# Residual additions, sums of squares and the last addition of a hybrid encoder step, moved from VectorE and GpSimd to accumulating DMAs

## The chip, the core and the metric

The kernel runs as one program on one core of a Trainium2 chip. The metric is device time in microseconds (us). The engines are named as the profile names them: PE is TensorE (matmul), DVE is VectorE, ACT is ScalarE, POOL is GpSimd, SP is SyncE, which only issues DMAs here. Each engine runs its own queue of instructions in order. A DMA is issued by one engine, which goes on to its next instruction, and it lands later.

## What is computed

One layer of a streaming encoder for 512 prompt tokens and 128 sample tokens (640 columns in all), width 2048. The parts that the change touches come after the mixer:

```
h = x + merged @ w_out
f = rms_norm(h, g_ffn)
h = h + (silu(f @ w_gate) * (f @ w_up)) @ w_down
gate = sigmoid(rms_norm(h, g_ple) @ w_ple_gate)
h = h + gate * (p_i @ w_ple_proj)
```

## The kernel before

Everything is held transposed: a tile has 128 features in its partitions and the 640 tokens in its free dimension, and a "pair" is two such tiles (128x2x640 float32, 640 KB). Pairs come from a pool of two buffers. DRAM scratch tensors (`h_dr`, `h2_dr`, `pj_dr`, `fc_dr`, `hc_dr`) hold what does not fit.

All large products are made by `strassen`: seven half-size products instead of eight, on float32 values that are cut into a high part (`wh`, `kf`) and a low remainder (`wl`). The work goes by weight units. A unit is one 512 KB load `wst` by SP. POOL makes three combinations of its blocks (lines L109, L110, L111 in `winograd_weights`), DVE a fourth (L112); ACT cuts the high part in two instructions (L86: one from `wst`, one from `ws`, the combinations), DVE subtracts to get the low part (L87), and PE runs 42 matmuls of 320 columns (L1205 to L1207). `ws` has one buffer and `wh` and `wl` two, so L109 of the next unit waits until L87 has read `ws`.

At the end of a product the seven sums are brought out of PSUM by ACT, DVE and POOL (L1232 to L1240). The last of these on DVE is L1239, which this text calls the last eviction.

The stages behind the mixer, in order:

- **Out-projection**, `o0` to `o7`, four units each. Behind each product: SP loads a pair of x, DVE adds it (L1280), ACT scales it by the gain (L1267, two instructions), POOL forms the combinations of the activations (L118 to L121), the pair goes to `h_dr`, ACT squares it (L1249) and DVE adds the two halves to a running sum `ssqa` (L1253, L1254).
- **Gate and up**, 22 times (`g`, `u`), eight units for both. After `g0` the sums of squares pass through two small matmuls `pm` over the partitions and a reciprocal root (`scale_rows`); after that `by_rows` multiplies every product by the row scale (L1257).
- **Down**, 28 cells: each of the eight pairs of h is built from several cells. The first 20 cells add their result to `h_dr` with an accumulating DMA issued by POOL (L1346). The last eight cells finish the pairs j = 4, 5, 6, 7 (three units each) and j = 0, 1, 2, 3 (two units each). Behind each, SP loads the pair from `h_dr`, DVE adds it (L1350), and scaling, combinations, squares and the write to `h2_dr` follow as in the out-projection.
- **Gate of the embedding**, `p0` to `p7`, four units each. After `p0` the row scale is made as above. Behind each of p0 to p6: `by_rows`, Sigmoid, the product with `pj` (L1370, DVE), a load of `hy` from `h2_dr`, its addition on POOL (L1373), and a write to the output `o_yT`.

The order of each engine's queue is chosen when the program is built, by a list scheduler of the framework that simulates the dependences; the code's order is only its input.

Of the kernel before, what the change touches and what calls it, by code (L numbers as in the profile page):

```python
# [9 lines left out]
F32 = mybir.dt.float32  # L10
# [4 lines left out]
OP = mybir.AluOpType  # L15
# [4 lines left out]
P = 128  # L20
D = 2048
KT = D // P
NTOK = 640
# [15 lines left out]
def halves(ap):  # L39
    return ap.rearrange("p (h n) -> p h n", h=2)  # L40
# [124 lines left out]
def hybrid_step(ctx: ExitStack, tc: tile.TileContext, io):  # L165
    nc = tc.nc
# [5 lines left out]
    dp = ctx.enter_context(tc.tile_pool(reuse_waits="tile", name="dram", bufs=1, space=DRAM))  # L172
# [22 lines left out]
    g_dr = dp.tile([1024, NTOK], F32, name="g_dr")  # L195
    m_dr = dp.tile([D, NTOK], F32, name="m_dr")
    h_dr = dp.tile([D, NTOK], F32, name="h_dr")
    h2_dr = dp.tile([D, NTOK], F32, name="h2_dr")
    tc_dr = dp.tile([FT // 2, P, 7, NH2], F32, name="tc_dr")
    fc_dr = dp.tile([KT // 2, P, 7, NH2], F32, name="fc_dr")  # L200
    hc_dr = dp.tile([KT // 2, P, 7, NH2], F32, name="hc_dr")
# [819 lines left out]
    for k in range(8):  # L1021
        t = gp_.tile([P, NTOK], F32, tag="xg", name=f"gld{k}", bufs=3)
# [4 lines left out]
    for k in range(2):  # L1027
        t = gp_.tile([P, NTOK], F32, tag="xg", name=f"p{k}", bufs=3)
# [3 lines left out]
    def row_scale(s, n, pm, y0, y2):  # L1032

        for i in range(2):
            nc.tensor.matmul(pm[i], ones, s[:, i * NH2 : (i + 1) * NH2], start=True, stop=True)
        for i in range(2):
            nc.vector.tensor_scalar(s[:, i * NH2 : (i + 1) * NH2], pm[i], 1.0 / n, EPS, op0=OP.mult, op1=OP.add)
        rsqrt(y0, y2, s, s)
# [7 lines left out]
    def rows(dram, j):  # L1046
        return dram[2 * j * P : 2 * (j + 1) * P, :].rearrange("(a p) n -> p a n", p=P)
# [92 lines left out]
    def bank(name):  # L1140
        return pc.tile([P, 512], F32, tag="p", name=name)

    def pair(name):
        return fo.tile([P, 2, NTOK], F32, tag="R", name=name, bufs=2)
# [19 lines left out]
    def seven(name):  # L1164
        return xp.tile([P, 7, NH2], F32, tag="c7", name=name, bufs=1)

    def keep(eng, c, dram, i):

        winograd_rows(eng, c[:, :4], c[:, 4:])
        nc.sync.dma_start(dram[i], c)  # L1170
# [72 lines left out]
    def scale_rows(s, n):  # L1243
        y = pair("y")
        pm = [bank(f"pm{i}")[:, :NH2] for i in range(2)]
        row_scale(s, n, pm, y[:, 0], y[:, 1])

    def squares(s, x, t, first, other=nc.vector):
        nc.scalar.activation(t, x, AF.Square)  # L1249
        if first:  # L1250
            nc.vector.tensor_tensor(s, t[:, 0], t[:, 1], op=OP.add)
        else:
            nc.vector.tensor_tensor(s, s, t[:, 0], op=OP.add)  # L1253
            other.tensor_tensor(s, s, t[:, 1], op=OP.add)  # L1254

    def by_rows(x, s):
        nc.vector.tensor_tensor(x, x, s[:, None, :].to_broadcast([P, 2, NTOK]), op=OP.mult)  # L1257
# [1 line left out]
    for i in range(5, 8):  # L1259
        s = seven(f"sm{i}")  # L1260
        mk.append(build(kp_tile(f"km{i}", i), pair(f"bm{i}"), s[:, 4:], m_dr, i, ssqs))
    ssqh, ssqp = ssqa, ssqs

    def scaled(c, x, gain, j):

        for a in range(2):
            nc.scalar.activation(c[:, 2 * a : 2 * a + 2], halves(x[:, a]), AF.Copy, scale=gain[:, 2 * j + a : 2 * j + a + 1])  # L1267

    fk = []
    for j in range(8):  # L1270
        after = None
        if j == 7:
            def after(u):
                for i in (2 * u, 2 * u + 1):
                    if i < 7:
                        fk.append(fetch(f"f{i}", i, fc_dr, i, nc.gpsimd if i == 3 else nc.vector, i == 6))
        r = strassen(f"o{j}", mk, after)
        x = pair(f"x{j}")
        nc.sync.dma_start(x, io["xT"][2 * j : 2 * j + 2].rearrange("a p n -> p a n"))
        nc.vector.tensor_tensor(r, r, x, op=OP.add)  # L1280
        c = seven(f"c{j}")
        scaled(c, r, gffn, j)
        if j < 7:
            keep(nc.gpsimd, c, fc_dr, j)
        else:
            winograd_rows(nc.gpsimd, c[:, :4], c[:, 4:])
            kf7 = kp_tile("kf7", 7)
            fk.append(kf7)
            later.setdefault(1, []).append(lambda: whole(kf7, c))
        nc.sync.dma_start(rows(h_dr, j), r)  # L1290
        squares(ssqh, r, x, j == 0)

    tk, slots = {}, (0, 1, 2, 3, 4, 5, 6, 7)

# [7 lines left out]
    for f in range(FT // 2):  # L1302
        z = strassen(f"g{f}", fk, cut_late if f == 0 else None)
        if f == 0:
            scale_rows(ssqh, D)
        by_rows(z, ssqh)
        nc.scalar.activation(z, z, AF.Silu)
        after = None
        if f == FT // 2 - 1:
            def after(u):  # L1310
                next_t(nc.gpsimd if u < 2 else nc.vector)
        c = seven(f"t{f}")
        t = c[:, :4].rearrange("p (a h) n -> p a (h n)", a=2)
        strassen(f"u{f}", fk, after, t)
        by_rows(t, ssqh)
        nc.vector.tensor_tensor(t, t, z, op=OP.mult)
        keep(nc.gpsimd, c, tc_dr, f)
# [14 lines left out]
    for n, (j, us, first, last) in enumerate(cells):  # L1332
        def after(i, us=us, n=n):
            uses[us[i]] -= 1
            if not uses[us[i]] and n < len(cells) - 8:
                next_t()
            if len(cells) - 4 <= n < len(cells) - 2:
                next_h()

        if n == len(cells) - 1:  # L1340
            def after(i):
                for _ in range(2 - i):
                    next_h()
        r = strassen(f"d{n}", [tk[i] for u in us for i in (2 * u, 2 * u + 1)], after)
        if not last:
            nc.gpsimd.dma_start(rows(h_dr, j), r, accum_op=OP.add)  # L1346
            continue
        x = pair(f"hx{j}")
        nc.sync.dma_start(x, rows(h_dr, j))
        nc.vector.tensor_tensor(r, r, x, op=OP.add)  # L1350
        c = seven(f"hc{j}")
        scaled(c, r, gple, j)
        if j != 3:
            keep(nc.gpsimd, c, hc_dr, j)
            ready.append(j)
        else:
            winograd_rows(nc.gpsimd, c[:, :4], c[:, 4:])
            hk[j] = whole(kp_tile("kh3", hslot[j]), c)
        nc.sync.dma_start(rows(h2_dr, j), r)
        squares(ssqp, r, x, j == 4)  # L1360
    hk = [hk[i] for i in (4, 5, 6, 7, 0, 1, 2, 3)]
    for j in range(7):
        z = strassen(f"p{j}", hk)
        if j == 0:
            scale_rows(ssqp, D)
        by_rows(z, ssqp)
        nc.scalar.activation(z, z, AF.Sigmoid)
        x = pair(f"pj{j}")
        nc.sync.dma_start(x, rows(pj_dr, j))
        nc.vector.tensor_tensor(z, z, x, op=OP.mult)  # L1370
        x = pair(f"hy{j}")
        nc.sync.dma_start(x, rows(h2_dr, j))
        nc.gpsimd.tensor_tensor(z, z, x, op=OP.add)  # L1373
        nc.sync.dma_start(rows(io["o_yT"], j), z)


    x = pair("pj7")
    y = seven("hy7")[:, :4].rearrange("p (a h) n -> p a (h n)", a=2)
    nc.sync.dma_start(x, rows(pj_dr, 7))
    nc.sync.dma_start(y, rows(h2_dr, 7))  # L1380
    ps = products("p7", hk, order=(1, 2, 6, 5, 3, 7, 4))
    z = pair("rp7")
    r11, r12, r21, r22 = blocks(z)
# [143 lines left out]
```

## Time and profile before

| | |
|---|---|
| median of three runs | 3040.45 us (3038.37 to 3044.05) |
| the profiled execution's own time | 3040.49 us |
| its span, first to last instruction | 3038.7 us |
| mean granted clock of TensorE | 0.977 of full speed |
| busy: PE | 2860.6 us, 94% of the span |
| busy: DVE | 2041.0 us, 67% |
| busy: POOL | 1541.0 us, 51% |
| busy: ACT | 1237.8 us, 41% |

A busy share is an average over stages with different limits, so the stages are also read one by one. Of the view by windows, each row names a stretch in us from the start of the span, then the busy time of each engine with the number of its instructions, then the granted clock, the busy share of the 16 DMA engines, and GB/s. The profiled execution ran 0.04 us from the median, so durations read from it can be set against the median as they are.

### The profile page before, as it was taken

Reading aid. Unit: us, or ns where it says so; the run is one execution under the profiler, and the core shown is the slowest. Engines: PE = TensorE matmul, PEld = TensorE weight load, DVE = VectorE, ACT = ScalarE, POOL = GpSimd, SP = SyncE. Lnnn points to the kernel's source line nnn. Section 1 sums busy time; section 2 is a strip of 40 time slices with the busy share of each in tenths; the row PEclk is TensorE's granted clock in tenths of the full one; section 3 lists DMA queues with packets and bytes.
Section 4 is the critical chain, followed back from the end, with each engine's and each line's share of the span. In section 5 each row is a group of like instructions: output and inputs, shape, how many; then the busy total and the mean of one; then the engine's idle time right before and its main releaser. Section 6 shows DMA issues by size and latency. Waiting matters only on the chain.

```text
span 3038.7 us, 48382 instructions
## 1 busy us (share of the span) xinstructions
PE 2860.6 (94%) x19051; PEld 2734.2 (90%) x19051; DVE 2041.0 (67%) x2827; ACT 1237.8 (41%) x1627; POOL 1541.0 (51%) x1548
## 2 busy tenths in 40 slices
PE   7899999999789889999999999999999999987898
PEld 6789988888788889999999999999889999987887
DVE  8949254454777786666666666666775666689666
ACT  4333365556633443333333333333434344344432
POOL 6512300000666665656565656565664555567555
PEclk9899999999899999999999999999999999999999
DMA  5465744456444623233333333332555455557343
GB/s 166 145 180 169 224 175 153 173 202 206 171 145 165 247 81 114 99 114 105 109 110 104 113 106 109 104 113 100 206 126 170 110 164 169 157 217 250 126 147 130
DMA packets 138069, 453.82 MB, mean 149 GB/s; under 512 B 14160, under 2 KB 34736, under 8 KB 124528
## 3 DMA queue, kind: packets, MB, share of 16 engines
q1 hardware_dynamic: 120608, 401.06, 38.7%
q0 software_dynamic: 15936, 45.47, 5.9%
q8 instruction: 149, 2.44, 0.3%
q10 hardware_dynamic: 1296, 4.20, 0.3%
q14 instruction: 80, 0.66, 0.1%
HBM read 344.55 MB, written 103.47 MB: 147 GB/s over the span
## 4 chain that ended last, share of the span: by engine, by line
POOL 22%; DVE 15%; PE 13%; issue 8%; ACT 5%; DMA 1%; DVEq 0%; POOLq 0%; SPq 0%; ACTq 0%
DVE wl L87 7%; POOL ws L110 7%; POOL ws L109 6%; ACT wh L86 5%; POOL ws L111 4%; PE d L1205 4%; PE d L1207 4%; PE d L1206 4%; POOL t L121 1%; DVE t L1257 1%; POOL t L118 1%; DVE rg L1257 1%; DVE kt L1051 1%; POOL rp L1373 1%; POOL t L119 1%
## 5 line engine op out<-in xcount | busy, mean ns | idle before, releaser
L87 DVE TENSOR_TENSOR wl<-ws,wh 128x1024 fp32r<-128x1024 f32 x328 | 418.9, 1277 | 468.7 <-ACT wh L86 468.5
L86 ACT ACTIVATE wh<-ws 128x1024 fp32r<-128x1024 f32 x328 | 347.1, 1058 | 946.4 <-POOL ws L111 933.9
L109 POOL TENSOR_TENSOR ws<-wst 128x256 f32<-128x256 f32 x328 | 335.4, 1022 | 760.8 <-DVE wl L87 758.3
L87 DVE TENSOR_TENSOR wl<-wst,wh 128x768 fp32r<-128x768 f32 x328 | 416.1, 1269 | 118.6 <-ACT wh L86 118.6
L1205 PE MATMUL d<-kt,wh 128*128 128x320 f32 x1232 | 387.8, 317 | 24.0 <-ACT wh L86 16.2
L1207 PE MATMUL g<-kf,wl 128*128 128x320 f32 x1232 | 380.3, 313 | 16.1 <-DVE wl L87 15.7
L86 ACT ACTIVATE wh<-wst 128x768 fp32r<-128x768 f32 x328 | 275.2, 839 | 274.0 <-PE d L1206 101.4
L1206 PE MATMUL d<-kt,wh 128*128 128x320 f32 x1232 | 385.8, 315 | 0.0
L1205 PE MATMUL g<-kf,wh 128*128 128x320 f32 x1232 | 382.1, 311 | 3.5 <-ACT wh L86 3.5
L1205 PE MATMUL u<-kf,wh 128*128 128x320 f32 x1232 | 380.6, 309 | 3.4 <-ACT wh L86 3.3
L1207 PE MATMUL d<-kt,wl 128*128 128x320 f32 x1232 | 366.4, 316 | 17.8 <-DVE wl L87 17.7
L1206 PE MATMUL g<-kf,wh 128*128 128x320 f32 x1232 | 381.4, 310 | 0.0
L1206 PE MATMUL u<-kf,wh 128*128 128x320 f32 x1232 | 380.3, 309 | 0.0
L1207 PE MATMUL u<-kf,wl 128*128 128x320 f32 x1232 | 379.5, 311 | 0.9 <-DVE wl L87 0.8
L110 POOL TENSOR_TENSOR ws<-ws,wst 128x256 f32<-128x256 f32 x328 | 353.4, 1078 | 23.4
L111 POOL TENSOR_TENSOR ws<-wst,ws 128x256 f32<-128x256 f32 x328 | 287.8, 878 | 21.2
L1205 PEld LDWEIGHTS d<-kt,wh 128*128 128x128 f32 x1232 | 238.1, 193 | 29.0 <-ACT wh L86 20.1
L1207 PEld LDWEIGHTS g<-kf,wl 128*128 128x128 f32 x1232 | 231.4, 189 | 23.0 <-DVE wl L87 22.4
L1207 PEld LDWEIGHTS d<-kt,wl 128*128 128x128 f32 x1232 | 231.3, 193 | 22.7 <-DVE wl L87 22.6
L1206 PEld LDWEIGHTS d<-kt,wh 128*128 128x128 f32 x1232 | 237.8, 193 | 0.0
L1205 PEld LDWEIGHTS g<-kf,wh 128*128 128x128 f32 x1232 | 232.5, 189 | 5.3 <-ACT wh L86 5.2
L1205 PEld LDWEIGHTS u<-kf,wh 128*128 128x128 f32 x1232 | 231.3, 188 | 4.2 <-ACT wh L86 4.2
(501 smaller groups left out, 6506.1 us busy)
## 6 DMA issues: line engine op xcount, KB each, us to landing
wst<-in_w_gate SPq DMA_DIRECT2D x88, 512.0 KB
wst<-in_w_up SPq DMA_DIRECT2D x88, 512.0 KB
wst<-in_w_down SPq DMA_DIRECT2D x88, 512.0 KB
tc_dr<-t SPq DMA_DIRECT2D x22, 1120.0 KB
kt<-tc_dr SPq DMA_DIRECT2D x22, 1120.0 KB
wst<-in_w_qk SPq DMA_DIRECT2D x32, 512.0 KB
kc<-in_cache_k SPq DMA_DIRECT2D x16, 1024.0 KB
vc<-in_cache_v SPq DMA_DIRECT2D x16, 1024.0 KB
```

The costliest lines, as they stand in the source:

```text
L86: a = nc.scalar.activation(wh[:, part], x, AF.Copy)
L87: b = nc.vector.tensor_tensor(wl[:, part], x, wh[:, part].bitcast(F32), op=OP.subtract)
L109: tt(s[:, 0], q[:, 0], q[:, 3], op=OP.add)
L110: tt(s[:, 1], s[:, 0], q[:, 1], op=OP.subtract)
L111: tt(s[:, 3], q[:, 2], s[:, 1], op=OP.subtract)
L118: tt(s[:, 0], q[:, 0], q[:, 1], op=OP.subtract)
L119: tt(q[:, 0], q[:, 2], q[:, 0], op=OP.subtract)
L121: tt(s[:, 2], s[:, 1], q[:, 3], op=OP.subtract)
L1205: nc.tensor.matmul(ps[i], wh[:, a, w], k[:, 0, b], start=f, stop=False)
L1206: nc.tensor.matmul(ps[i], wh[:, a, w], k[:, 1, b], start=False, stop=False)
L1207: nc.tensor.matmul(ps[i], wl[:, a, w], k[:, 0, b], start=False, stop=l)
L1257: nc.vector.tensor_tensor(x, x, s[:, None, :].to_broadcast([P, 2, NTOK]), op=OP.mult)
```

## The change

Three kinds of work leave the compute engines:

- **Residuals.** The pair from x, or from `h_dr`, is no longer loaded and added by DVE. POOL issues a DMA that adds it in place to the pair in SBUF (`residual`, L1282 after). Two of the sixteen, o7 and the cell of j = 3, keep a load by SP and an addition on DVE.
- **Sums of squares.** ACT still squares (L1251 after). The squared pair is added by a DMA, issued by POOL (L1255; the first of each series is plain, L1253), to a DRAM pair `sq_dr`. After `g0` and `p0` SP loads the sum (L1259) and DVE adds its two halves (L1260).
- **The last addition.** The second residual h is written straight to the output `o_yT` (pair 7 to `h7_dr`), and for p0 to p6 POOL issues a DMA that adds the gated embedding to it there (L1385). The loads of `hy`, the additions on POOL and the writes to `o_yT` are gone.

In all 37 DMAs are new on POOL's queue: 14 residuals, 16 of squares, 7 last additions. Line numbers of the changed kernel are one higher than before up to the squares, and more below.

```diff
-    def squares(s, x, t, first, other=nc.vector):
+    def squares(sums, x, t, first):
         nc.scalar.activation(t, x, AF.Square)
         if first:
-            nc.vector.tensor_tensor(s, t[:, 0], t[:, 1], op=OP.add)
+            nc.gpsimd.dma_start(sums, t)
         else:
-            nc.vector.tensor_tensor(s, s, t[:, 0], op=OP.add)
-            other.tensor_tensor(s, s, t[:, 1], op=OP.add)
+            nc.gpsimd.dma_start(sums, t, accum_op=OP.add)
+
+    def sum_rows(s, sums):
+        t = pair("sums")
+        nc.sync.dma_start(t, sums)
+        nc.vector.tensor_tensor(s, t[:, 0], t[:, 1], op=OP.add)
...
+    def residual(r, src, name, urgent):
+        x = pair(name)
+        if urgent:
+            nc.sync.dma_start(x, src)
+            nc.vector.tensor_tensor(r, r, x, op=OP.add)
+        else:
+            nc.gpsimd.dma_start(r, src, accum_op=OP.add)
+        return x
...
-        x = pair(f"x{j}")
-        nc.sync.dma_start(x, io["xT"][2 * j : 2 * j + 2].rearrange("a p n -> p a n"))
-        nc.vector.tensor_tensor(r, r, x, op=OP.add)
+        x = residual(r, io["xT"][2 * j : 2 * j + 2].rearrange("a p n -> p a n"), f"x{j}", j == 7)
...
-        squares(ssqh, r, x, j == 0)
+        squares(sq_dr[0], r, x, j == 0)
...
         if f == 0:
+            sum_rows(ssqh, sq_dr[0])
             scale_rows(ssqh, D)
...
-        x = pair(f"hx{j}")
-        nc.sync.dma_start(x, rows(h_dr, j))
-        nc.vector.tensor_tensor(r, r, x, op=OP.add)
+        x = residual(r, rows(h_dr, j), f"hx{j}", j == 3)
...
-        nc.sync.dma_start(rows(h2_dr, j), r)
-        squares(ssqp, r, x, j == 4)
+        nc.sync.dma_start(rows(io["o_yT"] if j < 7 else h7_dr, j % 7), r)
+        squares(sq_dr[1], r, x, j == 4)
...
         if j == 0:
+            sum_rows(ssqp, sq_dr[1])
             scale_rows(ssqp, D)
...
-        x = pair(f"hy{j}")
-        nc.sync.dma_start(x, rows(h2_dr, j))
-        nc.gpsimd.tensor_tensor(z, z, x, op=OP.add)
-        nc.sync.dma_start(rows(io["o_yT"], j), z)
+        nc.gpsimd.dma_start(rows(io["o_yT"], j), z, accum_op=OP.add)
```

The scheduler orders the queues anew. On POOL, in the middle of the out-projection, before the change (`ro` is the pair of the residual, `c` the scaled activations, `ws` the combinations of a weight unit):

```order
L111 TENSOR_TENSOR ws_8928<-wst_8827,ws_8928 128x256
L118 TENSOR_TENSOR c_8953<-c_8953 128x320
L109 TENSOR_TENSOR ws_9016<-wst_8882 128x256
L119 TENSOR_TENSOR c_8953<-c_8953 128x320
L120 TENSOR_TENSOR c_8953<-c_8953 128x320
L110 TENSOR_TENSOR ws_9016<-ws_9016,wst_8882 128x256
L121 TENSOR_TENSOR c_8953<-c_8953 128x320
L111 TENSOR_TENSOR ws_9016<-wst_8882,ws_9016 128x256
```

The same place on POOL after the change:

```order
L111 TENSOR_TENSOR ws_8927<-wst_8826,ws_8927 128x256
L1282 DMA ro_8938<-in_xT 128x2x640
L109 TENSOR_TENSOR ws_9013<-wst_8881 128x256
L110 TENSOR_TENSOR ws_9013<-ws_9013,wst_8881 128x256
L111 TENSOR_TENSOR ws_9013<-wst_8881,ws_9013 128x256
L118 TENSOR_TENSOR c_8951<-c_8951 128x320
L119 TENSOR_TENSOR c_8951<-c_8951 128x320
L120 TENSOR_TENSOR c_8951<-c_8951 128x320
L1255 DMA sq_dr_75<-x_8949 128x1280
```

The next unit's combinations now stand whole between the residual's DMA and the combinations of the activations; before, the two were interleaved.

On ACT at the same place, before (`wh` is the high part of a weight unit):

```order
L86 ACTIVATE wh_8926<-ws_8928 128x1024
L1267 ACTIVATE c_8953<-ro_8939,c_g_ffn 128x640 x2
L1249 ACTIVATE x_8950<-ro_8939 128x1280
L86 ACTIVATE wh_9014<-wst_8882 128x768
L86 ACTIVATE wh_9014<-ws_9016 128x1024
```

And on ACT after the change:

```order
L86 ACTIVATE wh_8925<-ws_8927 128x1024
L86 ACTIVATE wh_9011<-wst_8881 128x768
L1273 ACTIVATE c_8951<-ro_8938,c_g_ffn 128x640 x2
L1251 ACTIVATE x_8949<-ro_8938 128x1280
L86 ACTIVATE wh_9011<-ws_9013 128x1024
```

One half of the next unit's high part has moved ahead of the work on `ro`; the other half (from `ws`) still stands behind it.

On POOL in the last cells of the down-projection, where a cell has two units, after the change (`rd` is the cell's pair, `hc` its scaled activations):

```order
L1241 TENSOR_TENSOR rd_26267<-rd_26267,qd_26268 128x320
L109 TENSOR_TENSOR ws_26342<-wst_26204 128x256
L110 TENSOR_TENSOR ws_26342<-ws_26342,wst_26204 128x256
L111 TENSOR_TENSOR ws_26342<-wst_26204,ws_26342 128x256
L1282 DMA rd_26267<-h_dr 128x2x640
L118 TENSOR_TENSOR hc_26280<-hc_26280 128x320
L109 TENSOR_TENSOR ws_26397<-wst_26265 128x256
L119 TENSOR_TENSOR hc_26280<-hc_26280 128x320
L120 TENSOR_TENSOR hc_26280<-hc_26280 128x320
L110 TENSOR_TENSOR ws_26397<-ws_26397,wst_26265 128x256
L1255 DMA sq_dr_76<-hx_26278 128x1280
L121 TENSOR_TENSOR hc_26280<-hc_26280 128x320
```

Here L118 follows the residual's DMA directly, with no other work of POOL between them. Before, the same place has L1240, the three of `ws`, L118 and the rest in the same order, without the two DMAs.

## Rows read from the trace of the kernel before

**Rows 1.** The page: busy times, and the chain that ended last by engine.

```profile
PE 2860.6 (94%) x19051; PEld 2734.2 (90%) x19051; DVE 2041.0 (67%) x2827; ACT 1237.8 (41%) x1627; POOL 1541.0 (51%) x1548
...
POOL 22%; DVE 15%; PE 13%; issue 8%; ACT 5%; DMA 1%; DVEq 0%; POOLq 0%; SPq 0%; ACTq 0%
```

**Rows 2.** Windows: gate/up, out-projection, three-unit cells, two-unit cells, p0, p2 to p7.

```profile
core 0: us, PE busy (x) PEld busy (x) DVE busy (x) ACT busy (x) POOL busy (x), PEclk, DMA share, GB/s
1130.00:1500.00 370.00, 365.27 (x2464) 361.09 (x2463) 250.92 (x284) 125.83 (x152) 223.87 (x223) 1.00 0.32 109
889.00:1029.00 140.00, 128.90 (x852) 124.62 (x851) 99.84 (x108) 53.49 (x65) 89.37 (x86) 1.00 0.46 164
2662.00:2731.00 69.00, 60.57 (x379) 58.01 (x378) 54.69 (x57) 31.58 (x38) 44.29 (x42) 0.95 0.62 226
2731.00:2795.00 64.00, 52.44 (x323) 49.99 (x321) 57.97 (x62) 30.59 (x38) 48.56 (x41) 0.95 0.66 234
2795.00:2842.00 47.00, 36.95 (x200) 35.23 (x200) 37.48 (x36) 24.72 (x27) 25.38 (x22) 0.85 0.50 166
2879.00:3019.00 140.00, 131.40 (x851) 124.43 (x849) 92.24 (x101) 45.49 (x55) 85.51 (x72) 1.00 0.44 144
```

**Rows 3.** Timeline of POOL behind p2 and p3: start, us, instruction, idle before.

```profile
2906.47 0.98 POOL L109 TENSOR_TENSOR ws<-wst 128x256 f32<-128x256 f32 x1 [2.43 <-DVE wl L87]
2907.41 3.68 POOL L1373 TENSOR_TENSOR rp<-rp,hy 128x1280 f32<-128x1280 f32 x1
2911.05 0.74 POOL L110 TENSOR_TENSOR ws<-ws,wst 128x256 f32<-128x256 f32 x1
...
2935.41 3.68 POOL L1373 TENSOR_TENSOR rp<-rp,hy 128x1280 f32<-128x1280 f32 x1
```

**Rows 4.** Groups of POOL, 2830 to 3030 us: busy, mean ns, idle before.

```profile
L1373 POOL TENSOR_TENSOR rp<-rp,hy 128x1280 f32<-128x1280 f32 x7 | 25.0, 3576 | 0.0
```

**Rows 5.** The accumulating DMA of the down-projection, line L1346: issue and landing.

```profile
L1346 POOL DMA_DIRECT2D h_dr<-rd x20: 1195/1204/1297, 2219.6 to 2648.0; - x20
...
DMA to landing us min/median/max: 6.2/7.9/9.5
```

**Rows 6.** Timeline of DVE in one period of the out-projection.

```profile
917.10 0.49 DVE L1239 TENSOR_TENSOR ro<-ro,o 128x320 f32<-128x320 f32 x1
917.68 1.49 DVE L1280 TENSOR_TENSOR ro<-ro,x 128x1280 f32<-128x1280 f32 x1
```

**Rows 7.** Timeline of ACT in the same period.

```profile
919.21 1.55 ACT L1267 ACTIVATE c<-ro,c_g_ffn 128x640 f32<-128x640 f32 x2 [0.87 <-DVE ro L1280]
920.67 1.26 ACT L1249 ACTIVATE x<-ro 128x1280 f32<-128x1280 f32 x1
...
927.76 1.06 ACT L86 ACTIVATE wh<-ws 128x1024 fp32r<-128x1024 f32 x1 [5.10 <-POOL ws L111]
```

**Rows 8.** Timeline of POOL in the same period.

```profile
920.12 0.94 POOL L118 TENSOR_TENSOR c<-c 128x320 f32<-128x320 f32 x1 [2.87 <-ACT c L1267]
...
927.00 0.73 POOL L111 TENSOR_TENSOR ws<-wst,ws 128x256 f32<-128x256 f32 x1
930.16 1.39 POOL L109 TENSOR_TENSOR ws<-wst 128x256 f32<-128x256 f32 x1 [2.43 <-DVE wl L87]
```

**Rows 9.** Timeline of POOL in the cell of j = 1.

```profile
2772.30 0.94 POOL L118 TENSOR_TENSOR hc<-hc 128x320 f32<-128x320 f32 x1 [4.13 <-ACT hc L1267]
...
2778.43 1.45 POOL L111 TENSOR_TENSOR ws<-wst,ws 128x256 f32<-128x256 f32 x1
2779.84 0.87 POOL L1240 TENSOR_TENSOR rd<-rd,qd 128x320 f32<-128x320 f32 x1
```

**Rows 10.** Timeline of DVE: last evictions of j = 7 and j = 3, and p0.

```profile
2730.45 0.47 DVE L1239 TENSOR_TENSOR rd<-rd,d 128x320 f32<-128x320 f32 x1
...
2794.46 0.47 DVE L1239 TENSOR_TENSOR rd<-rd,d 128x320 f32<-128x320 f32 x1
...
2803.28 1.48 DVE L1350 TENSOR_TENSOR rd<-rd,hx 128x1280 f32<-128x1280 f32 x1
...
2808.57 1.49 DVE L1253 TENSOR_TENSOR ssq<-ssq,hx 128x640 f32<-128x640 f32 x1
...
2811.39 1.49 DVE L1254 TENSOR_TENSOR ssq<-ssq,hx 128x640 f32<-128x640 f32 x1
```

**Rows 11.** Waits, 2795 to 2842 us: total, times, longest.

```profile
PE p L1205 <- ACT wh L86: 6.9, 4, 3.3
PE p L1207 <- DVE wl L87: 3.1, 1, 3.1
```

More of the change, by code (lines that the diff above doesn't have):

```diff
@@ L197, in hybrid_step @@
     h_dr = dp.tile([D, NTOK], F32, name="h_dr")
-    h2_dr = dp.tile([D, NTOK], F32, name="h2_dr")
+    h7_dr = dp.tile([2 * P, NTOK], F32, name="h7_dr")
+    sq_dr = [dp.tile([P, 2, NTOK], F32, name=f"sq_dr{i}") for i in range(2)]
     tc_dr = dp.tile([FT // 2, P, 7, NH2], F32, name="tc_dr")
@@ L1379, in hybrid_step @@
     nc.sync.dma_start(x, rows(pj_dr, 7))
-    nc.sync.dma_start(y, rows(h2_dr, 7))
+    nc.sync.dma_start(y, rows(h7_dr, 0))
     ps = products("p7", hk, order=(1, 2, 6, 5, 3, 7, 4))
```

## The prediction

> **What bounds the kernel now.** The page comes first: PE is busy for 94% of the span, yet of the chain that ended last only 13% is PE's and 22% is POOL's [rows 1]. PE is fed without slack, and in places POOL decides when. To find the places I take the windows, stage by stage, and divide time by matmuls [rows 2]. Gate and up runs 2464 matmuls in 370 us, 150.2 ns each, so 168 matmuls (four units) take 25.2 us; this is my floor for PE at full clock. The out-projection takes 164.3 ns, 27.6 us per 168. The last part of the gate stage takes 164.5 ns, again 27.6. So both stages lose 2.4 us per product to something else. The two-unit cells take 198 ns per matmul and p0 takes 235, at clocks of 0.95 and 0.85. Gate/up, half of the kernel, is not touched; the change can gain only in the stages that run above the floor.
>
> The timelines of POOL and ACT then say what the loss is. Behind p2, the addition L1373 takes 3.68 us and stands between L109 and L110 of a weight unit [rows 3]; there are seven, 3.58 us in the mean, with no idle time ahead of them [rows 4]. POOL's next L109 waits for L87, which waits for ACT, which waits for POOL's L111: a ring in which every POOL instruction counts. In the out-projection, the last eviction ends at 917.59 and the addition L1280 follows at once [rows 6]; then ACT's scaling and squares, POOL's L118 to L121 with the next unit between them until 927.73 [rows 8], and only then ACT's `wh` at 927.76, ready at 928.82 [rows 7]. From eviction to weights it is 11.23 us.
>
> **The change, part by part.** The sum is made against the profiled execution's own time, 3040.49 us, which is 0.04 above the median; no correction is needed.
>
> *Last addition, p0 to p6.* The addition of 3.68 us leaves POOL, and an issue of an accumulating DMA comes: 1.20 us by the nearest rows [rows 5]. That frees 2.48 us of each period, and the floor lets 27.6 fall to 25.2: 2.4 us. DMA L1385 needs the product with `pj`, which is done long before (L1373 had no idle time), so it adds no wait. The end of the DMA is waited for by nothing soon; of the seven I count six, since p7 follows another order: 6 x -2.4 = **-14.5**. The bounds: if the issue takes as long as the addition, 0; if each of seven gains 2.4, -17.
>
> *Residuals in the out-projection.* No row shows an accumulating DMA into SBUF. The nearest is L1346, the same 640 KB added by POOL's queue, but in DRAM: issue to landing 6.2 at least, 7.9 in the median, 9.5 at most [rows 5]. I take 7.9. The Trainium skill, "DMA: Bandwidth & Descriptors", section "Anatomy of one DMA — SWDGE (gpsimd) path", gives such a DMA about 2.0 us and its bytes at 436 GB/s, so 3.5 us here as an estimate, and says that most of the fixed part is the confirmation of the write, longest for HBM. By that each residual would be 4.4 us shorter; L1346 took more than twice the page's value, so the row stands. The new path by the order: last eviction, DMA 7.9, ACT's two scalings and the square until `wh` can start, 2.72 (919.21 to 921.93 [rows 7]), and 1.06 for `wh`. With 0.1 of gaps this is 11.8 against 11.23. POOL's three of the next unit lie inside the landing, and L118 to L121 behind `wh` instead of ahead of it. So +0.6 for each of seven: **+4**. The issue of the squares (1.2) lies where POOL waits 2.43 for L87 [rows 8], so it costs nothing; without that cover it would be 7 x 1.2 = +8. The additions L1253 and L1254 leave DVE, which has 40 of 140 us idle there [rows 2]: no gain.
>
> *Three-unit cells, j = 4, 5, 6.* The same exchange at the same length, 3 x 0.6: **+2**. The high DMA share (0.62) speaks for a longer landing, which belongs to the range.
>
> *Two-unit cells.* Here POOL has nothing between the DMA and L118, so its walk is a chain: landing 7.9, one scaling 0.8 (half of 1.55 [rows 7]), L118 to the end of L111, 2772.30 to 2779.88 = 7.6, the issue for the squares 1.2, L1240 0.87 [rows 9]. That makes 18.4 per cell. The four accumulating cells j = 7, 0, 1, 2 lie between the last eviction of j = 7 and that of j = 3, now 2730.92 to 2794.93, 64.0 us [rows 10]. 4 x 18.4 = 73.6: **+10**. The bounds: 0 if the landing of 6.2 and DVE's relief (it is busy 58 of 64 us [rows 2]) cancel it; +17 at a landing of 9.5.
>
> *p0.* The stretch from the last eviction of j = 3 takes 47 us for 200 matmuls, which the floor's rate would do in 30: 17 us lost. DVE is the late one: L1350 of j = 3 starts 8.35 us after its eviction, behind cuts of other tiles, and L1253 and L1254 take 2.98 more [rows 10]. PE waits 10.0 us for ACT and DVE [rows 11]. The two additions go, the row scale moves to the end of p0 with its matmuls, and with later cells the cuts will be done before j = 3 is. I take **-10**, between 0 (the waits move to the `pm` matmuls behind a late load of the sum) and -15 (nearly all of the loss).
>
> *From the out-projection to the gate.* DVE loses two additions of squares, like those of rows 10 and so 3 us, where it also cuts tiles. In return the load for o7 stands behind two other loads of SP, and the sum of squares is loaded before the scale. The cover of that load is g0's 25.2 us; without it PE stops at `pm` for a landing or so. I take **0**, within 6 either way.
>
> The sum: -14.5 + 4 + 2 + 10 - 10 + 0 = -8.5, so 3040.49 - 8.5 = **3032 us**.
>
> **The rivals.** *Slower: the landing.* The fourteen residuals lie on the path, so each microsecond of landing costs 14 us. At 9.5 instead of 7.9 that is 14 x 1.6 = +22, and the time is 3054. It decides from 7.9 + 8.5 / 14 = 8.5 us on. For it: seven of them fall into stretches with a DMA share of 0.62 to 0.66, and these DMAs also read what they add to. Against it: L1346 landed in 7.9 beside gate and down traffic.
>
> *Faster: a short landing.* At 6.2 us it is 7 x -1.7 = -12 in the out-projection, and of as much again in the cells I count half, since DVE is nearly full there [rows 2]: -18, and 3014. For it: the destination is SBUF, and a write to SBUF may be confirmed sooner; against it: L1346 has 6.2 as its shortest of twenty. The rule of the Trainium skill, "DMA: Bandwidth & Descriptors", same section, would lead here, with a still shorter landing of 3.5 us as an estimate; the trace so far doesn't bear it out.
>
> *The tail's gain does not come.* If p0 stays as long as now, because PE's wait moves from `wh` to the scale of the rows (one landing of the last square's DMA, SP's load and the root in sequence), the -10 is gone: 3042, no change. For it: all squares must land before `sum_rows`, where before the sum was at hand in SBUF. Against it: p0's matmuls, 25.2 us at the floor, lie ahead of it.
>
> *The change does nothing in the gate stage.* If the ring of L109, L87 and L86 sets 27.6 by itself, -14.5 is lost: 3046. Against it: in the ring with L1373 POOL is busy 85.5 of 140 us and still has only 2.4 us idle at a time, and gate/up runs the same ring at the floor.
>
> **Chances.** The forecast 0.40; the long landing 0.23; the short one 0.17; the tail's gain gone 0.13; no gain in the gate stage 0.07. A measurement of this kernel can tell about 0.2%, 6 us, from no change. The forecast's own range is 3022 to 3042, some of it within 6 us of 3040; so faster by over 0.2%: 0.31 of the forecast and the short landing 0.17, 0.48. Slower: the long landing 0.23, 0.05 of the gate case, and 0.04 where several terms are at their dear ends, 0.32. The same: 0.20. The range reaches from 3012, below the short landing, to 3056, above the long one.
>
> **What would show it.** In the gate stage the starts of L1385 should lie 25.2 us apart instead of 28.0 (2907.41 to 2935.41 [rows 3]). The landing of L1282 should be near 7.9, and ACT's L1273 the one that waits for it; the out-projection's rate should stay near 164 ns. The evictions of the last cells should spread to 18.4 us. p0 should run at under 200 ns a matmul. The prediction is wrong if L1282 lands far from 7.9, if issues of POOL take more than 1.2, or if PE stops at `pm`.

## The result, and the profile after

The changed kernel is slower: 3062.25 us in the median of four runs (3056.74 to 3066.83), against 3041.32 for the kernel before beside it; the ratio is 1.0077, with a 95% interval of 1.0064 to 1.0091. The prediction was 3032. Its rival of a long landing had 3054 and the right sign. The profiled execution is the slowest of the four, 3066.83 us with a span of 3064.7, so stages read from it sum to 26 us over [rows 1]'s execution and not to 21.

To see where the 26 us lie, take the end of the last eviction of each product (L1239 before, L1240 after) in both traces and subtract. Lengths in us:

| stretch between last evictions | before | after | difference |
|---|---|---|---|
| up to o0 | 864.95 | 866.27 | +1.3 |
| o0 to o7, out-projection | 199.62 | 216.30 | +16.7 |
| o7 to the last down cell before j = 4 | 1583.03 | 1585.34 | +2.3 |
| cells j = 4, 5, 6, 7 (three units) | 83.32 | 95.99 | +12.7 |
| cells j = 0, 1, 2, 3 (two units) | 64.01 | 91.03 | +27.0 |
| p0 | 46.08 | 27.53 | -18.6 |
| p1 to the end of the span | 197.70 | 182.21 | -15.5 |

The windows of the same stages in the changed kernel (gate/up, out-projection, three-unit cells, two-unit cells, p0, p2 onward; the columns are those of [rows 2]):

```profile
1150.00:1520.00 370.00, 366.26 (x2479) 363.35 (x2479) 250.28 (x283) 126.09 (x152) 223.59 (x223) 1.00 0.32 109
894.00:1044.00 150.00, 132.48 (x832) 130.12 (x831) 80.44 (x90) 52.11 (x66) 90.54 (x95) 0.93 0.64 175
2682.00:2764.00 82.00, 64.56 (x386) 62.22 (x385) 43.89 (x49) 29.83 (x37) 46.90 (x48) 0.88 0.72 214
2764.00:2855.00 91.00, 59.94 (x346) 56.61 (x345) 51.51 (x58) 37.96 (x45) 54.82 (x55) 0.83 0.84 240
2855.00:2883.00 28.00, 25.35 (x152) 23.98 (x151) 21.54 (x23) 15.97 (x19) 13.26 (x12) 0.93 0.56 175
2906.00:3046.00 140.00, 139.26 (x939) 137.40 (x937) 101.99 (x114) 52.89 (x63) 82.28 (x79) 1.00 0.52 139
```

Against [rows 2], the last stage runs 939 matmuls where it ran 851, gate/up is as it was, and the out-projection and the cells run fewer matmuls per us, less work on DVE, and at a lower granted clock: 1.00 has become 0.93, and 0.95 has become 0.88 and 0.83. DVE and POOL are less busy there than before and PE waits more, so it is not an engine that is full. The chain that ended last now has transfers in it:

```profile
PE 31%; POOL 24%; DVE 20%; issue 10%; DMA 8%; ACT 7%; POOLq 0%; DVEq 0%; SPq 0%; ACTq 0%
```

DMA was 1% [rows 1]. The view of the new line L1282, the accumulating residual, says whom it keeps waiting:

```profile
L1282 POOL DMA_DIRECT2D ro<-in_xT x7: 1207/1212/1304, 866.9 to 1044.3; - x7
L1282 POOL DMA_DIRECT2D rd<-h_dr x7: 1207/1209/1477, 2682.5 to 2824.2; - x7
...
  ACT c L1273: 48.7, 7
  ACT hc L1273: 39.0, 6
...
DMA to landing us min/median/max: 6.5/8.8/15.2
```

The issue costs POOL 1.21 us, as assumed [rows 5]. But ACT stands idle 88 us for the landings, and ACT's queue also holds the high parts of the weights. One period of the out-projection shows it. Timeline of ACT in the changed kernel, at the place of [rows 7]:

```profile
924.55 0.85 ACT L86 ACTIVATE wh<-wst 128x768 fp32r<-128x768 f32 x1
932.55 1.55 ACT L1273 ACTIVATE c<-ro,c_g_ffn 128x640 f32<-128x640 f32 x2 [7.16 <-DMA ro<-in_xT]
934.01 1.25 ACT L1251 ACTIVATE x<-ro 128x1280 f32<-128x1280 f32 x1
935.17 1.04 ACT L86 ACTIVATE wh<-ws 128x1024 fp32r<-128x1024 f32 x1
```

And PE in the same period:

```profile
931.93 0.31 PE L1208 MATMUL o<-km,wl 128*128 128x320 f32 x1
936.26 0.42 PE L1206 MATMUL o<-km,wh 128*128 128x320 f32 x1 [4.02 <-ACT wh L86]
...
938.35 0.47 PE L1206 MATMUL o<-km,wh 128*128 128x320 f32 x1
938.62 0.47 PE L1207 MATMUL o<-km,wh 128*128 128x320 f32 x1
```

The combinations for that unit were ready at 929.10 (POOL's L111, 928.36 and 0.74). ACT could have cut them 6 us earlier; they stood behind two scalings and a square that waited for a DMA. After the stop the matmuls are spaced 0.27 us instead of 0.15 for some 3.5 us: the granted clock is at the lower of its two levels, 1.2 GHz (0.51 of full speed from 937.3 to 940.7), after a stop of 4 us. The unit takes 11.99 us where 6.16 is its length without a stop.

In the last cells the same wait blocks something else. PE, ACT and SP at the end of the cell of j = 2, one fence each:

```profile
2833.62 0.31 PE L1208 MATMUL p<-kh,wl 128*128 128x320 f32 x1
2847.58 0.64 PE L1206 MATMUL p<-kh,wh 128*128 128x320 f32 x1 [13.65 <-ACT rd L1235]
```

```profile
2839.45 1.55 ACT L1273 ACTIVATE hc<-rd,c_g_ple 128x640 f32<-128x640 f32 x2 [8.25 <-DMA rd<-h_dr]
...
2847.11 0.41 ACT L1235 ACTIVATE rd<-d 128x320 f32<-128x320 f32 x1
```

```profile
2821.88 0.33 SPq L60 DMA_DIRECT2D wst<-in_w_pg  x1
2825.60 2.06 SPq L1183 DMA_DIRECT2D kh<-hc_dr  x2
2828.43 0.33 SPq L60 DMA_DIRECT2D wst<-in_w_pg  x1
2839.44 0.39 SPq L1372 DMA_DIRECT2D o_yT<-rd  x1
```

The residual was issued at 2824.18 and landed at 2839.43, 15.25 us later, beside two reloads of 1120 KB that SP issued from 2825.60 on and a weight load. ACT's eviction of the next cell (L1235) stands behind the scaling, so the PSUM bank that p0 needs is not free, and PE stops for 13.65 us. Not all of this is the residual's: with all residuals on DVE and the squares by DMA (the second experiment below) PE stops at the same place for 5.24 us.

The fourteen landings of that execution, sorted by what SP issued from 6 us before a residual until it landed:

| beside it | landing, us |
|---|---|
| one weight load (512 KB) issued 0.5 us before it or earlier | 6.5, 6.8, 6.9, 7.1 |
| only a write of 1120 KB, issued 4.8 us before | 8.0 |
| one weight load at the same moment | 8.2, 8.7, 9.0, 9.0, 9.0 |
| a write and a reload of 1120 KB and two weight loads | 11.6 |
| two reloads of 1120 KB and a weight load or more | 13.8, 14.5, 15.2 |

The mean is 8.9 in the out-projection and 10.3 in the cells. The ten without a reload beside them have a mean of 7.9, the four with one 13.8.

### The profile page after: what moved, and what is told of

The parts are those of the page before. It is cut to its first block, busy times and chain, and to the rows that moved or that the text cites. A ratio compares the mean times of both kernels' runs of the same rounds, so it can differ in the third digit from the quotient of the medians.

```text
span 3064.7 us, 48366 instructions
## 1 busy us (share of the span) xinstructions
PE 2864.2 (93%) x19051; PEld 2744.0 (90%) x19051; DVE 1979.4 (65%) x2785; ACT 1237.7 (40%) x1627; POOL 1521.8 (50%) x1578
## 4 chain that ended last, share of the span: by engine, by line
PE 31%; POOL 24%; DVE 20%; issue 10%; DMA 8%; ACT 7%; POOLq 0%; DVEq 0%; SPq 0%; ACTq 0%
DVE wl L87 8%; POOL ws L110 7%; PE qk L746 7%; POOL ws L109 7%; ACT wh L86 5%; POOL ws L111 5%; PE d L1208 4%; PE d L1206 4%; PE d L1207 4%; DMA rd<-h_dr 2%; DMA ro<-in_xT 2%; PE acc L513 1%; PE acc L512 1%; PE acc L511 1%; POOL t L121 1%
## 5 line engine op out<-in xcount | busy, mean ns | idle before, releaser
L87 DVE TENSOR_TENSOR wl<-ws,wh 128x1024 fp32r<-128x1024 f32 x328 | 428.6, 1307 | 540.2 <-ACT wh L86 539.6
L109 POOL TENSOR_TENSOR ws<-wst 128x256 f32<-128x256 f32 x328 | 333.1, 1016 | 754.4 <-DVE wl L87 754.4
L87 DVE TENSOR_TENSOR wl<-wst,wh 128x768 fp32r<-128x768 f32 x328 | 410.1, 1250 | 140.1 <-ACT wh L86 140.1
L1208 PE MATMUL d<-kt,wl 128*128 128x320 f32 x1232 | 369.4, 316 | 15.3 <-DVE wl L87 15.1
L110 POOL TENSOR_TENSOR ws<-ws,wst 128x256 f32<-128x256 f32 x328 | 357.5, 1090 | 24.5
L111 POOL TENSOR_TENSOR ws<-wst,ws 128x256 f32<-128x256 f32 x328 | 278.0, 848 | 22.1
L1208 PEld LDWEIGHTS u<-kf,wl 128*128 128x128 f32 x1232 | 231.3, 188 | 3.9 <-DVE wl L87 1.3
```

The source lines that it names most:

```text
L87: b = nc.vector.tensor_tensor(wl[:, part], x, wh[:, part].bitcast(F32), op=OP.subtract)
L109: tt(s[:, 0], q[:, 0], q[:, 3], op=OP.add)
L110: tt(s[:, 1], s[:, 0], q[:, 1], op=OP.subtract)
L111: tt(s[:, 3], q[:, 2], s[:, 1], op=OP.subtract)
L1208: nc.tensor.matmul(ps[i], wl[:, a, w], k[:, 0, b], start=False, stop=l)
```

## The experiments

The kernel before ran on the same chip beside each group of them; its medians were 3038.6 to 3041.3, so a few us between kernels of different groups say nothing.

**Only the last addition.** The kernel before with this edit (its other lines write the second residual straight to `o_yT`, pair 7 to `h7_dr`):

```diff
-        x = pair(f"hy{j}")
-        nc.sync.dma_start(x, rows(h2_dr, j))
-        nc.gpsimd.tensor_tensor(z, z, x, op=OP.add)
-        nc.sync.dma_start(rows(io["o_yT"], j), z)
+        nc.gpsimd.dma_start(rows(io["o_yT"], j), z, accum_op=OP.add)
```

> The kernel before with only the last addition (p0 to p6) done by an accumulating DMA into the output. Theory R (the residuals' landings cost some 40 us net, the last addition gives back 17, the squares nothing): periods of the gate stage at 24.9 instead of 27.9 us, all other stages as before, 3041 - 17 = 3024. Rival S (the squares' DMAs cost as well, or the gain of the gate stage needs the squares off DVE): the gate stage stays above 26.5 us per period, 3033 or more.

Measured: 3019.25 us (3018.98 to 3022.0), ratio 0.9938 [0.9921, 0.9954]. The periods of the gate stage are 24.9 us, every stage ahead of it is as before within 1.2 us. So the last addition alone gives 20 us, and its gain needs no other part of the change.

**Residuals back on DVE, squares and last additions by DMA.** The changed kernel with every residual urgent:

```diff
-        x = residual(r, ..., f"x{j}", j == 7)
+        x = residual(r, ..., f"x{j}", True)
...
-        x = residual(r, rows(h_dr, j), f"hx{j}", j == 3)
+        x = residual(r, rows(h_dr, j), f"hx{j}", True)
```

> The changed kernel with all sixteen residuals loaded by SP and added by DVE, as before; squares and last additions stay accumulating DMAs. Theory R: out-projection back to 27 to 28 us per period, cells back to their old spacings, last additions still worth 17: 3022 to 3028. Rival S (the squares' DMAs on POOL's queue share in the loss): 3035 to 3045, with the out-projection above 28.5 us per period.

Measured: 3011.82 us (3004.29 to 3013.55), ratio 0.9906 [0.9889, 0.9922]. Better than either expectation: the residuals cost the changed kernel 50 us, and the squares do not cost but gain 7.5 beside the last addition. Windows of this kernel for the out-projection, the two kinds of cells, and p0:

```profile
892.00:1024.00 132.00, 125.06 (x829) 121.18 (x828) 79.66 (x94) 53.92 (x65) 83.25 (x88) 1.00 0.61 198
2660.00:2727.00 67.00, 61.84 (x394) 59.09 (x394) 47.03 (x53) 30.44 (x37) 41.47 (x45) 0.97 0.75 262
2727.00:2801.00 74.00, 56.33 (x330) 52.98 (x328) 56.12 (x62) 37.01 (x45) 52.93 (x52) 0.87 0.82 269
2801.00:2830.00 29.00, 26.52 (x157) 25.14 (x157) 21.44 (x24) 15.72 (x18) 13.48 (x13) 0.91 0.63 211
```

The out-projection is below both other kernels, 26.2 us in most periods, with a granted clock of 1.00. By last evictions the changed kernel loses 29.8 us against it from o0 to o7, gets 6.0 of that back until the last cells, loses 31.7 in the cells and gains 1.0 in p0; with the 1.6 us by which it reached o0 earlier that is the 52.9 between the two spans. p0 takes 28.6 us here, so its fall from 46.1 to 27.5 does not need the residuals' DMAs.

**Only the residuals.** The kernel before with the function `residual` and its two calls, nothing else changed.

> The kernel before with only the fourteen residuals done by accumulating DMAs. Theory R: 3041 + 38 = 3079, between 3070 and 3085, with ACT waiting about 8 us for each landing. Rival S: about half of the loss is the squares', so 3055 to 3065.

Measured: 3071.89 us (3066.89 to 3073.15), ratio 1.0105 [1.009, 1.012]: +33, in the range of the first theory and outside that of the rival. ACT waits 45.2 us in the out-projection and 37.6 in the cells, about as in the changed kernel. By last evictions, against the kernel before: o0 to o7 grows by 18.0 us and the cells by 35.1, while p0 shrinks by 23.0 (46.08 to 23.10), though no squares have moved. That p0 has this to give back here, and not beside the squares, is most of the difference between 33 and 50.

**Only the squares.** The kernel before with `squares` and `sum_rows` of the changed one.

> The kernel before with only the sums of squares done by accumulating DMAs. The run with only the last addition took 3019 and the run with squares and last addition 3012; if the parts add up, the squares alone give 3039 - 7.5 = 3032, with the out-projection at about 26.2 instead of 27.7 us per period. If the squares help only beside the other part, 3039 within 4.

Measured: 3025.45 us (3019.45 to 3031.37), ratio 0.9954 [0.994, 0.9969]. The squares alone give 13 us (9 to 18 by the interval); whether that is more than the 7.5 beside the last addition these few runs do not settle. By last evictions, against the kernel before: o0 to o7 shrinks by 13.9 us, 5.7 of it is lost again until the last cells, the cells grow by 8.0, p0 shrinks by 16.6 (46.08 to 29.50), and p1 to the end grows by 1.1. So the squares alone end the long p0 of before, as the residuals alone do.

**Residuals by DMA in one place only.** The changed kernel with DVE adding in the cells, and then with DVE adding in the out-projection.

> The changed kernel with accumulating DMAs for the residuals of the out-projection only; those of the last cells are loaded by SP and added by DVE. Theory: the loss of the residuals is the sum of the two places. Out-projection as in the changed kernel (30.4 us per period), worth 22 us over the version with all residuals on DVE: 3012 + 22 = 3034, and the cells from j = 4 to j = 3 as in that version. Rival: the loss sits in one place, so 3015 or 3058.

> The changed kernel with accumulating DMAs for the residuals of the last cells only; those of the out-projection are loaded and added by DVE. Theory: the other part of the sum, 3012 + 28 = 3040, with the out-projection at 26.2 us per period and the cells as in the changed kernel. Rival: 3015 or 3058, the mirror image of the run with the out-projection only.

Measured: 3032.81 us (3026.54 to 3037.07), ratio 0.9978 [0.9967, 0.9988], and 3036.33 us (3031.57 to 3041.81), ratio 0.9993 [0.9984, 1.0003]. Over the kernel with DVE in both places the out-projection's cost 21 and the cells' 24.5. That is within 4 us of the expectation in both; the sum of 45.5 leaves 5 of the 50 over, which is within what these runs scatter.

**Where the wait stands.** The changed kernel with the work on a finished pair behind the next product's second unit:

```diff
+    def late_tail(u):
+        if u == 1 and tails:
+            f = tails.pop()
+            with tc.issue_after(ring.done[0]), tc.issue_after(ring.done[1]):
+                f()
...
-        scaled(c, r, gffn, j)
...
+        def tail(j=j, r=r, x=x):
+            c = seven(f"c{j}")
+            scaled(c, r, gffn, j)
...
+            tails.append(tail)
```

> The changed kernel, but the work on a finished pair (scaling, combinations, write, squares) is put behind the cut of the next product's second-next weight unit; the residual's DMA is issued where it was. Theory Q (the cost is not the DMA itself but that ACT's queue stands still behind the scaling until it lands): out-projection falls from 30.4 to 25.5 to 27 us per period, the last cells shrink by 10 to 25 us, 3062 falls to 3015 to 3035, while the landings stay at 7 to 15 us. Rival T (the residual's DMA takes the DMA engines from the weight loads, or slows POOL and DVE): the periods stay near 30 us, 3050 or more.

Measured: 3034.8 us (3026.07 to 3036.33), ratio 0.9977 [0.9967, 0.9986]: 27 us of the 50 are back, at the upper edge of the first theory. In the traces o0 to o7 is 11.3 us shorter than in the changed kernel and the cells 15.0. The landings are what they were, and ACT's wait for them has shrunk from 48.7 and 39.0 us:

```profile
  ACT hc L1273: 16.9, 6
  ACT c L1273: 10.3, 5
...
DMA to landing us min/median/max: 6.4/8.8/14.8
```

The rival (traffic by itself) falls as the main cause. The expected period does not hold throughout: 29.1 and 30.1 in o2 and o3, 25.4 and 24.6 in o4 and o5, 32.4 in o6. The cells of two units gain nothing (90.8 us against 91.0), and PE stops for 12.8 us ahead of p0, much as in the changed kernel; that two units are too little work to stand ahead of a landing of 14.8 us is the likely reason, not a tested one.

**The same order with the cells on DVE, and with all on DVE.** These two tell what the DMA costs when its wait is covered.

> Residuals by DMA in the out-projection only, with the work on a finished pair put behind the cut of the second-next unit there and in the cells; the cells add on DVE. Theory Q (the landing costs only what ACT's queue stands still for): with the landing covered the out-projection falls from 30 to 25 to 27 us per period and the time from 3033 (without that order) to 3010 to 3020, within 6 of the same order with all residuals on DVE. Rival T (the DMA's traffic costs by itself): above 3022, and 10 or more above the version with DVE.

> The same order of work as in the run before it, with all sixteen residuals loaded by SP and added by DVE; squares and last additions by DMA. If the order helps by itself, the out-projection falls from 26.2 towards 25.2 us per period and 3012 to 3000 to 3008; if the weight ring is all that is left there, 3012 within 5.

Measured: 3025.25 us (3024.18 to 3031.76), ratio 0.9958 [0.9943, 0.9973], and 3018.8 us (3016.6 to 3022.95), ratio 0.9936 [0.992, 0.9953]. With the changed kernel's own order the residuals of the out-projection cost 21 us; with the covered order 6.5, and ACT's wait for them falls from 44.8 to 6.9 us. Most of their price is this wait and what stands behind it. The 6.5 lies between the two theories' marks (6, and 10 or more). Both expected times were missed: 3025 lies among the rival's times, and 3019 lies above both of its own ranges, since the order costs the last cells 8.6 us (163.9 against 155.4 in the kernel with DVE and the old order). In the out-projection it gains DVE's version no shorter period (27 to 28.6 us); what it loses there comes back before the last cells, which it reaches 5.9 us earlier.

**What the landing is made of.** First the layout: the scratch of h kept by pairs, so that a partition's values are one run of 5120 bytes.

```diff
-    h_dr = dp.tile([D, NTOK], F32, name="h_dr")
+    h_dr = [dp.tile([P, 2, NTOK], F32, name=f"h_dr{i}") for i in range(8)]
...
-        x = residual(r, rows(h_dr, j), f"hx{j}", j == 3)
+        x = residual(r, h_dr[j], f"hx{j}", j == 3)
```

> The changed kernel with the DRAM scratch of the first residual kept by pairs, so that each partition's 1280 values lie together (5120 bytes, as in the squares' DMAs, whose landing is 6.0 us) instead of two runs of 2560. Theory D (the layout of the rows sets the length of the accumulating DMA): the landing of the twenty additions of the down cells falls from 8.0 to about 6 us, that of the residuals in the cells by about 2 us, 3062 falls by about 14 to 3048. Rival C (other transfers beside it set it): the twenty stay near 8 us, the cells' residuals at 7 to 15 us, 3062 within 6.

Measured: 3053.14 us (3047.85 to 3054.65), ratio 1.0045 [1.003, 1.006]. The twenty additions of the down cells (their line is L1361 here), in this kernel and then in the changed one:

```profile
L1361 POOL DMA_DIRECT2D h_dr<-rd x20: 852/859/867, 2236.9 to 2666.3; - x20
...
DMA to landing us min/median/max: 5.9/7.8/8.7
```

```profile
L1361 POOL DMA_DIRECT2D h_dr<-rd x20: 1184/1188/1209, 2239.3 to 2668.4; - x20
...
DMA to landing us min/median/max: 6.2/8.0/9.6
```

The issue on POOL falls from 1.19 to 0.86 us, the landing hardly: in these twenty, most of which have only weight loads beside them, the layout does not set it, so the first theory falls. The rival does not hold as it stands either: the kernel gains 9 us, a time between the two expectations, and this comes with the landings beside reloads: the three that took 14.5, 11.6 and 15.2 us took 8.9, 10.8 and 11.1. Why long runs suffer less there was not tried further.

Then the neighbours: the reloads of kh held back on SP's queue until the last pair is written, and so until its residual is in.

```diff
-            hk[i] = fetch(f"h{i}", hslot[i], hc_dr, i)
+            with tc.issue_after(wrote[-1].ins):
+                hk[i] = fetch(f"h{i}", hslot[i], hc_dr, i)
...
-        nc.sync.dma_start(rows(io["o_yT"] if j < 7 else h7_dr, j % 7), r)
+        wrote.append(nc.sync.dma_start(rows(io["o_yT"] if j < 7 else h7_dr, j % 7), r))
```

> The changed kernel, but SP issues the 1120 KB reloads of kh only behind the write of the last finished pair, so not while that pair's residual is on its way. Theory C (a residual's landing is as long as the loads that SP issues beside it make it: 6.5 to 7.1 us alone, 8 to 9 beside one 512 KB weight load, 11.6 to 15.2 beside reloads): the three long landings of the cells, 14.5, 11.6 and 15.2 us, fall to 7 to 9 us and 3062 to 3044 to 3052. Rival D (the accumulating DMA from the scratch is slow by itself, at times): the landings keep 11 to 15 us at the same places, 3062 within 6 or slower, since the reloads come later.

Measured: 3054.14 us (3046.84 to 3055.89), ratio 1.0044 [1.0029, 1.0059]. The seven residuals of the cells in this kernel, by the line's view of that stretch:

```profile
L1282 POOL DMA_DIRECT2D rd<-h_dr x7: 1207/1207/1216, 2678.4 to 2812.1; - x7
...
  ACT hc L1273: 27.2, 6
...
DMA to landing us min/median/max: 6.4/8.6/10.9
```

The landings of 14.5 and 15.2 us are 8.7 and 8.6 now; the one of 11.6 is 10.9, with two weight loads beside it. So the reloads made the long ones, with the same DMA and the same layout. The cells shrink from 187.0 to 166.7 us, but the reloads' cuts now fall into p0, which grows from 27.5 to 39.2 (PE stops there for 6.7 us at `pm`, for the sum of squares, and for 4.9 at `kh`), and 8 us remain of the gain, a little less than expected.

**A version meant to beat both.** Residuals on DVE, the new order in the out-projection only.

> A version meant to beat both: all residuals on DVE, squares and last additions by DMA, the work on a finished pair behind the cut of the second-next unit in the out-projection only and at once in the last cells. In the runs so far that order reached the last cells 6 us earlier and lost 8.5 us inside them. If the two places are independent, 3012 - 6 = 3006; if the cells' spacings depend on how they are entered, 3012 to 3019.

Measured: 3010.07 us (3007.23 to 3014.07), ratio 0.9903 [0.9886, 0.9919]. It lies between its two expectations. It beats both kernels, but not measurably the one with DVE's residuals and the old order (0.9906): it reaches the last cells 4.4 us earlier in its profile and shows 3 us of that at the end. What counts here is to keep two of the three parts, the squares and the last addition.

## Why the prediction was wrong, by its steps

**Right, with luck in the total: the last addition.** -14.5 was predicted and the stretch from p1 to the end shrank by 15.5; the run with this part alone gave 20. DMAs L1385 start 24.8 us apart (2944.17 after 2919.38). The floor from gate/up was a little high, so a period gained 3.0 us where 2.4 was taken. That the total fits so well is luck: the five periods behind p1 gave 16.4 us where five times 2.4 is 12, and p1 itself took 2.4 longer than before. The rival that the ring holds the stage at 27.6 is out.

**Failed: the residuals, at two steps.** The terms +4, +2 and +10 make 16; the runs say 50 against DVE with the rest of the change, and 33 against the kernel before.

*In the out-projection, the path that ended at `wh`.* The prediction summed from the last eviction to `wh`, 11.8 us against 11.23, and put what comes behind it at nothing. The run with only the residuals shows that this fails even where the sum holds. Behind o1 to o5 its landings were 6.7 to 7.9 us and `wh` ended 10.9 to 12.2 us behind the last eviction, as summed; yet the periods took 29.4 to 30.7 us, against 27.1 to 28.7 before. Behind o2, where the last eviction ends at 923.31 and `wh` at 935.15, DVE and POOL go on like this in that run:

```profile
934.23 1.47 DVE L1253 TENSOR_TENSOR ssqa<-ssqa,x 128x640 f32<-128x640 f32 x1 [7.02 <-ACT x L1249]
935.74 1.39 DVE L1254 TENSOR_TENSOR ssqa<-ssqa,x 128x640 f32<-128x640 f32 x1
937.05 1.21 DVE L87 TENSOR_TENSOR wl<-ws,wh 128x1024 fp32r<-128x1024 f32 x1
...
938.34 1.39 POOL L109 TENSOR_TENSOR ws<-wst 128x256 f32<-128x256 f32 x1 [1.90 <-DVE wl L87]
```

ACT's square had waited for the landing too, so DVE's two additions now stand between `wh` and L87, and POOL's next L109 waits for L87. It starts 15.03 us behind the eviction, where it started 12.57 behind it before (930.16 [rows 8]). From there to the next eviction it is 15.3 us in both kernels: the 2.5 us by which L109 came later are the whole growth of the period. The prediction had named this ring (L109 waits for L87, which waits for ACT), but ended its sum before the ring closes.

In the changed kernel the additions have left DVE, and two other things make L109 late. `wh` ends 13.3 us behind the eviction (922.95 to 936.21), where the sum gave 11.8. And L87 behind it takes 2.65 us (2.64 to 2.68 in all five of these periods, 1.23 before), so L109 starts 16.0 us behind the eviction. DVE and POOL after the change, then DVE at the same place before it:

```profile
936.24 2.65 DVE L87 TENSOR_TENSOR wl<-ws,wh 128x1024 fp32r<-128x1024 f32 x1 [8.55 <-ACT wh L86]
...
938.97 1.38 POOL L109 TENSOR_TENSOR ws<-wst 128x256 f32<-128x256 f32 x1 [1.17 <-DVE wl L87]
```

```profile
928.85 1.23 DVE L87 TENSOR_TENSOR wl<-ws,wh 128x1024 fp32r<-128x1024 f32 x1 [2.56 <-ACT wh L86]
```

POOL's last combination (L121), which the prediction moved behind `wh` at no price, and its issue of the squares' DMA run in that time; what makes L87 longer is not shown. PE's stop also costs more than its length: 4.0 us idle became 5.8 us of a unit with the clock at 1.2 GHz behind it. The periods grew by up to 3.3 us. The comparison itself was off as well: without the squares on DVE a period takes 26.2, not 27.6.

*In the cells, the landing, "I take 7.9".* It was taken from L1346. That row has weight loads beside it, as the residuals have (all of the down-projection, none of the gate's, which the prediction named too): eleven of its twenty were issued within 0.6 us of one and took 8.05 us in the median, five had one 0.8 us before them or earlier and took 6.2 to 6.8. Four had two reloads behind them, but only 4.2 us later, and took 7.8 to 8.9. The ten residuals without a reload agree with the row; what it does not hold is a reload issued together with the DMA, and the four residuals beside reloads took 13.8 in the mean. By the prediction's own price the measured means give 7 x (8.9 - 7.9) + 7 x (10.3 - 7.9) = 24 us, slightly more than the rival's 22. The DMA share of 0.62 to 0.66 was named as that rival's ground; it should have been the forecast's. The Trainium skill, "DMA: Bandwidth & Descriptors", section "Issuing engines are not separate DMA queues", says that transfers of all issuing engines run interleaved on the same sixteen DMA engines. The trace agrees: 6.5 to 15.2 us for the same 640 KB by what SP had issued.

With the reloads held back the cells come near the prediction's sums: 84.6 us with three units, where its terms give 85.3, and 82.1 with two, where they give 79.6 with the 9.4 us that those four landings took in the mean. So the chain of the cells was nearly right, and its landing was mis-sized; the sum also left out that ACT's queue, with evictions in it, stands still as long (PE's stop of 13.65 us). The prediction's bound of +17 for these cells, at a landing of 9.5, comes out as +16 from its own terms.

**Failed with the sign of the sum: the squares in the out-projection, "no gain".** They gave 13.9 us from o0 to o7 in the run that moves nothing else. DVE's 40 idle us of 140 did not mean that its additions were free. Which of the two brings it, DVE's relief or the new order of ACT and POOL, is not separated.

**Right in place, the cause not separated: p0.** It fell by 18.6 us where 10 was taken. The squares alone make it fall by 16.6, with 8.0 us more in the cells, and the residuals alone by 23.0, with 35.1 more in the cells. That fits what the prediction said of later cells, that the cuts are then done before j = 3 is; but then part of the work had only moved, and the gain should not be counted apart from the cells. Of the rival that PE would stop at `pm` the changed kernel shows 0.6 us.

**Small.** From the out-projection to the gate, +2.3 where 0 within 6 was taken. The issues of POOL are as assumed for the residuals and the last additions (1.21 and 1.19 us) and shorter for the squares (0.86).

## What to carry to other kernels

An accumulating DMA in place of an addition is worth it where nobody waits for its end: the last addition into the output gave 20 us and the sums of squares 13. Where the next step needs the result at once, its landing is a wait in the queue of the engine that takes it, and everything behind that instruction waits too; look for what is queued there before the durations are summed, and follow the sum until the ring closes, not only to the first result. Take the landing from a row with the same neighbours: the loads that are issued at the same moment as the DMA are part of its price.

## What the runs showed of the hardware that was not expected

A plain DMA of 640 KB from SBUF to DRAM on POOL's queue (L1253, the first of the squares) landed after 3.3 us, and the same with accumulation (L1255) after 6.0 in the median:

```profile
L1255 POOL DMA_DIRECT2D sq_dr<-x x7: 862/871/903, 905.6 to 1101.9; - x7
L1255 POOL DMA_DIRECT2D sq_dr<-hx x7: 846/859/879, 2717.4 to 2867.4; - x7
...
DMA to landing us min/median/max: 5.8/6.0/12.1
```

The rule of the Trainium skill, "DMA: Bandwidth & Descriptors", section "Anatomy of one DMA — SWDGE (gpsimd) path", which the prediction put at 3.5 us by its formula, fits the plain DMA here. The accumulating ones took at least 2.3 us longer than this estimate in this execution, into DRAM (shortest 5.8) and into SBUF (shortest residual 6.5) alike.

The issue on POOL differs with the addition and with the length of the contiguous runs in DRAM: 0.58 and 0.61 us for the plain one in runs of 5120 bytes, 0.86 for accumulation in runs of 5120 bytes, 1.19 to 1.21 in runs of 2560.
